# Layer 0: the second half's first norm moved to the start, the first half's output and cross attention moved beside the second half's attentions, the memories moved

## The chip, the core and the metric

The kernel runs on one core of a Trainium2 chip. Five engines work side by side and meet only through semaphores: PE (matmuls, with its weight loads PEld), DVE (vector work), ACT (activations), POOL (GpSimd) and SP, which here only issues DMAs. Each engine takes its instructions strictly in the order in which they stand in its queue. The metric is the device time of one execution in microseconds (us).

## What is computed

Two layers of a decoder for 1024 tokens of width 1024, all in fp32. What matters here is layer 0, cut to its main lines:

```python
x = x + mixers[0](rms_norm(x, mix_norm))                   # w_in, two attentions, w_out
x = x + memory_cross_attention(rms_norm(x, x_norm), rms_norm(mem, mem_norm), wq, wkv, wo)
x = x + swiglu(rms_norm(x, ffn_norm), wg, wu, wd)
...
z = h @ w_in                                               # even_mixer
qa, ka, va, cq, ckv, kr = jnp.split(z, EVEN_SPLITS, axis=-1)
oa, _ = banded_attention(rope(qa), rope(ka), va, SWA_WINDOW - 1, sink=sinks)
qb = (rms_norm(cq, q_norm) @ w_uq)                         # q_nope, q_rope (rope'd)
kvb = (rms_norm(ckv, kv_norm) @ w_ukv)                     # k_nope, vb
ob = causal_mla_attention(q_nope, q_rope, k_nope, k_rope, vb)
return jnp.concatenate([oa, ob], axis=-1) @ w_out
```

The cross attention has 4 heads over 256 memory tokens. Layer 1 has another attention and the same cross attention and SwiGLU.

## The kernel before

**Halves and streams.** The tokens are worked in two halves of 512 (A, `hf` 0, and B, `hf` 1). A causal attention of half B needs the keys and values of half A, so A can run ahead of B. All of the code is recorded as Python generators that yield how much PE work they have just recorded, in units of one 128x512 matmul. `weave(main, fill, ratio)` (line 341, `g_weave` line 293) takes turns: for each unit of `main` it lets `fill` record `ratio` units; a `Gap(n)` in `main` asks for at least n units of `fill` there (it stands for a latency that something must cover), and `Until(cond)` lets `fill` run until a mark is set. A scheduler then orders each engine's queue, starting from the order of recording. `scaled(g, f)` multiplies what a generator yields by f, and `DENSE` (0.05) marks parts that need next to no fill.

There are two streams with buffers of their own: S (`self.S`, names that begin with s) for the latency-bound work, with 5 of the 8 PSUM banks, and D (`self.D`, names with d) for dense projections, with 3 PSUM banks, 2 raw weight buffers and 3 pairs of weight slots `wh`/`wl`. Every product is made of three matmuls: operands are split into a high and a low part. For a weight block (128x1024) SP loads `wr`, ACT copies it to `wh` (line 212), POOL subtracts to get `wl` (line 181). For activations DVE does the subtraction (`lo`, line 181).

**Names.** `proj0_units(hf)` (line 991) is the projection of layer 0 for one half: `w_in`, the two latent norms (lines 1037 and 1052 are their two matmuls with ones), `w_ukv`, `w_uq`. `g_swa(hf)` (line 1210) is the sliding-window attention: scores line 1254, transposes 1278, values 1285 and 1286. `g_mla(hf)` (line 1309) with `g_heads` (line 822) is the latent attention of 8 heads: scores 749, softmax on DVE 758 to 767 and ACT 762, transposes 785, values 796 to 799. `g_rest(l, hf)` (line 881) is what follows: `w_out` (names `oh`, `ol`), a norm, the cross attention (`xq`, lines 942 to 968), `w_xo`, and the norm for the FFN. `g_accum` (line 645) adds each 128x512 product to x on DVE (line 660). `memory_units(l)` (line 564) makes keys and values of the memory for layer l (`mxn`, `mem`). `norm_b` (in `body`) is half B's first norm: load `xB`, squares on ACT, reciprocal root on DVE, `xn` on DVE (line 416), 32 transposes on PE (line 399). `g_ffn` (line 676) is the SwiGLU (`hfh`, `hfl`; DVE lines 687, 691, 181 and 660).

**Order of layer 0 before.** Two weaves.

1. `sparse`: `g_swa(0)`, `norm_b`, `g_mla(0)`, `g_rest(0, 0)`, all on S, with `dense` as fill on D: `proj0_units(0)` with the first two of the memory units of layer 0 inside it, the rest of these, then, after half B's norm, `proj0_units(1)` and the memory units of layer 1.
2. `first0`: `g_swa(1)`, `g_mla(1)`, `g_rest(0, 1)` on S, with half A's `g_ffn(0)` as fill on D at 1.6.

Layer 1 follows in two more weaves with the FFN of the other half as fill, and half B's last FFN runs alone.

Of the kernel before, what the change touches and what calls it, by code (L numbers as in the profile page):

```python
# [18 lines left out]
P = 128  # L19
# [24 lines left out]
R0, R1, R2, R3, R4 = 1.5, 1.6, 1.6, 2.3, 2.1  # L44
# [118 lines left out]
class Builder:  # L163
# [400 lines left out]
    def memory_units(self, l, s):  # L564
# [5 lines left out]
        def load():  # L570
            for b in range(2):
                xn.append(self.A4.tile([P, D], F32, tag="a4", name="mxn"))
                nc.sync.dma_start(xn[b], I["mem"][0, b * P:(b + 1) * P, :])
            return self.gain(f"l{l}_mem_norm")
# [14 lines left out]
        def norm(_):  # L589
# [3 lines left out]
            for b in range(2):  # L593
                yield from self.g_turn(s if l else self.S, xn[b], lambda k0: tuple(t[:, k0:k0 + 4, b * P:(b + 1) * P] for t in mv))
# [227 lines left out]
    def g_heads(self, s, m, hf, heads, bias, scale):  # L822
# [5 lines left out]
        def flush():  # L828
# [6 lines left out]
            if g % 2:  # L835
                self.att_out(m, ot, self.OTd[row0:row0 + 64, hf * 512:(hf + 1) * 512])
# [21 lines left out]
    def att_mem(self, hf, ext, rope, sets=None):  # L858
# [14 lines left out]
        if rope:  # L873
            m.qr = ring(2, 512) if hf else Ring([ext.tile([P, 512], F32R, name=f"qr{i}") for i in range(2)])
        m.ph = Ring([ext.tile([P, 512], F32R, name=f"ph{i}") for i in range(2)])
# [5 lines left out]
    def g_rest(self, l, hf, x, xsrc, out):  # L881

        nc, I, st, s = self.nc, self.I, self.st, self.S
        ts = slice(hf * 512, (hf + 1) * 512)
        if x is None:
            x = self.xtile("x")
            with self.hold(HOLD):
# [5 lines left out]
        def out_proj():  # L893
            with ExitStack() as es:
                o = self.pool(es, f"op{l}{hf}", 2)
                for c in range(4):
                    h = o.tile([P, 1024], F32R, tag="oh", name="oh")
                    lo = o.tile([P, 1024], F32R, tag="ol", name="ol")
                    with self.hold(HOLD):
                        self.split_in(s, h, lo, [(lambda raw: raw.rearrange("p (k t) -> p k t", t=512),  # L900
                                                  self.OTd[c * 256:(c + 1) * 256, ts].rearrange("(k p) t -> p k t", p=P))], "dve", nc.gpsimd)
# [3 lines left out]
        yield from self.scaled(out_proj(), DENSE)  # L905
# [4 lines left out]
        with ExitStack() as es:  # L910
# [9 lines left out]
            yield from self.scaled(self.units([q_unit(h) for h in range(4)]), DENSE)  # L920
# [51 lines left out]
            s.apart = True  # L972
# [9 lines left out]
            for c in range(2):  # L982
                yield from self.scaled(self.g_accum(s, [(q[:, 2 * c + j, 0], q[:, 2 * c + j, 1]) for j in range(2)],
                                                    I[f"l{l}_w_xo"], c * 256, x, after if c else None), DENSE)
# [6 lines left out]
    def proj0_units(self, hf, tab, s, given, mem=None):  # L991
# [190 lines left out]
        first = s if mem is None else self.S  # L1182
        qa = [(cols(pr * P), roped(self.to_queries(pr, hf), first if pr < 2 else s)) for pr in range(4)]
        if mem is None:
            yield cols(640), va
        yield cols(512), roped(self.to_keys(0, hf), first)
        if mem is not None:
            yield next(mem)
        yield from qa[0:2]
        if mem is not None:  # L1190
            yield next(mem)
# [12 lines left out]
        yield sq  # L1204
        yield q_nope(0)
# [562 lines left out]
```

## Time and profile before

| | us |
|---|---|
| median of 3 runs | 2974.36 (2972.03 to 2979.24) |
| the profiled execution, whole | 2978.69 |
| its span in the profile | 2976.7 |
| PE busy | 2819.6 (95%) |
| PEld, DVE, POOL, ACT busy | 2350.7, 1790.7, 1478.8, 1309.3 |
| granted PE clock, mean over the span | 0.973 |

The profile is one execution. "Busy" counts the time in which an engine has an instruction under way; matmuls overlap, so PE busy is not PE at its peak. The granted clock is 1.0 at 2.4 GHz and 0.5 at 1.2 GHz; a mean between says for what share of the stretch each was granted. A row of waits names the instruction that waited, and what came last of what it waited for.

### The profile page before, as it was taken

What the parts mean: (1) busy time and instruction counts of PE and PEld (TensorE: products, weight loads), DVE (VectorE), ACT (ScalarE), POOL (GpSimd) and SP (SyncE); (2) the same over time, 40 slices, a digit from 0 to 9 for tenths busy, and PEclk for the clock granted to TensorE, in tenths of its full rate; (3) what the DMA queues carried; (4) which work ended last, traced back from release to release, by engine and by line L of the source; (5) the groups of instructions that cost most, each with busy time, mean ns of one, the idle gap of its engine ahead of it and who ended that gap; (6) DMA issues with size and microseconds to landing.
All of it is one profiled execution on the core that took longest, in us unless ns stands there. A gap on an engine that the chain in (4) does not pass through costs nothing. (4 is left out here: it accounts for less than half of the span.)

```text
span 2976.7 us, 37929 instructions
## 1 busy us (share of the span) xinstructions
PE 2819.6 (95%) x13500; PEld 2350.7 (79%) x13500; DVE 1790.7 (60%) x3668; ACT 1309.3 (44%) x2539; POOL 1478.8 (50%) x1070
## 2 busy tenths in 40 slices
PE   6878998899999999999999999999999999999998
PEld 5666777787888887888888787877888878788887
DVE  5784766566765556346776646346888765652234
ACT  4654534454443343265544334356655533432222
POOL 3475544663444444554656344455665644444442
PEclk9987999999999999999999999999999999999999
DMA  5665644643434323464555333465555443333331
GB/s 168 179 209 175 210 140 133 165 142 106 143 122 132 122 86 123 136 203 152 160 151 174 106 107 107 141 199 169 170 157 148 154 144 111 92 121 99 92 100 63
DMA packets 385216, 417.61 MB, mean 140 GB/s; under 512 B 32964, under 2 KB 295364, under 8 KB 385028
## 3 DMA queue, kind: packets, MB, share of 16 engines
q1 hardware_dynamic: 333124, 245.67, 27.9%
q0 software_dynamic: 51904, 169.52, 17.3%
q8 instruction: 107, 1.75, 0.2%
q14 instruction: 81, 0.66, 0.1%
HBM read 347.09 MB, written 68.03 MB: 139 GB/s over the span
## 5 line engine op out<-in xcount | busy, mean ns | idle before, releaser
L181 POOL TENSOR_TENSOR wl<-wr,wh 128x1024 fp32r<-128x1024 f32 (+1 forms) x430 | 1039.6, 2425 | 913.6 <-ACT wh L212 864.1
L212 ACT ACTIVATE wh<-wr 128x1024 fp32r<-128x1024 f32 (+1 forms) x418 | 440.1, 1056 | 738.9 <-PE d L236 248.2
L236 PE MATMUL d<-hfh,wh 128*128 128x512 f32 x1408 | 559.1, 398 | 5.8 <-DVE x L660 5.8
L236 PE MATMUL d<-hfh,wl 128*128 128x512 f32 x1408 | 553.9, 394 | 0.0
L236 PE MATMUL d<-hfl,wh 128*128 128x512 f32 x1408 | 553.4, 393 | 0.0
L236 PE MATMUL d<-wh,a 128*128 128x512 f32 x1440 | 528.3, 398 | 10.4 <-DVE ra L360 3.0
L660 DVE TENSOR_TENSOR x<-d,x 128x512 f32<-128x512 f32 x344 | 234.3, 687 | 299.8 <-PE d L236 298.8
L236 PEld LDWEIGHTS d<-wh,a 128*128 128x128 f32 x1440 | 272.4, 190 | 69.4 <-issue 6.6
L236 PEld LDWEIGHTS d<-hfh,wh 128*128 128x128 f32 x1408 | 266.7, 189 | 55.2 <-issue 4.4
L236 PEld LDWEIGHTS d<-hfh,wl 128*128 128x128 f32 x1408 | 265.7, 189 | 53.0
L236 PEld LDWEIGHTS d<-hfl,wh 128*128 128x128 f32 x1408 | 266.5, 189 | 49.5
L236 PE MATMUL d<-wl,a 128*128 128x512 f32 x720 | 283.2, 395 | 0.0
L660 DVE TENSOR_TENSOR x<-s,x 128x512 f32<-128x512 f32 x192 | 130.6, 689 | 113.1 <-PE s L236 111.8
L181 DVE TENSOR_TENSOR a<-t,a 128x512 fp32r<-128x512 f32 x104 | 164.3, 1580 | 31.2 <-ACT a L693 28.4
L236 PEld LDWEIGHTS d<-wl,a 128*128 128x128 f32 x720 | 136.9, 190 | 24.3
L762 ACT ACTIVATE af<-af,nm 128x512 f32<-128x512 f32 (+3 forms) x160 | 94.1, 589 | 110.5 <-DVE nm L758 100.3
L181 DVE TENSOR_TENSOR pl<-s,ph 128x512 fp32r<-128x512 f32 (+1 forms) x158 | 97.7, 631 | 46.7 <-ACT ph L184 46.0
L184 ACT ACTIVATE ph<-s 128x512 fp32r<-128x512 f32 (+1 forms) x158 | 83.9, 551 | 83.7 <-PE s L785 80.1
L687 DVE SCALAR_TENSOR_TENSOR t<-t,d 128x512 f32<-128x512 f32 x88 | 60.2, 684 | 98.3 <-ACT t L686 97.8
L236 PE MATMUL s<-hmh,wl 128*128 128x512 f32 x256 | 100.7, 393 | 3.9 <-POOL wl L181 3.9
L399 PE MATMUL s<-ident,xn 128*128 128x128 f32 x384 | 62.8, 310 | 41.9 <-DVE xn L416 39.1
L236 PE MATMUL s<-hml,wh 128*128 128x512 f32 x256 | 100.3, 392 | 0.0
(360 smaller groups left out, 5690.3 us busy)
## 6 DMA issues: line engine op xcount, KB each, us to landing
wr<-in_l_w_gate SPq DMA_DIRECT2D x88, 512.0 KB
wr<-in_l_w_up SPq DMA_DIRECT2D x88, 512.0 KB
wr<-in_l_w_down SPq DMA_DIRECT2D x88, 512.0 KB
wr<-in_l_w_qkv SPq DMA_DIRECT2D x48, 512.0 KB
wr<-in_l_w_out SPq DMA_DIRECT2D x32, 512.0 KB
tab<-qd POOLq DMA_DIRECT2D x32, 512.0 KB, 5.6
ar<-qd POOLq DMA_DIRECT2D x24, 512.0 KB, 7.4
wr<-in_l_w_in SPq DMA_DIRECT2D x22, 512.0 KB
```

What stands on the lines that cost most here:

```text
L181: e.tensor_sub(out, x, h.bitcast(F32))
L184: self.nc.scalar.activation(h, ps, AF.Copy)
L212: self.nc.scalar.activation(h, raw, AF.Copy)
L236: self.nc.tensor.matmul(ps, a, b, start=(3 * i + j == 0), stop=(3 * i + j == n - 1))
L399: self.nc.tensor.transpose(v[:, k, :], xn[:, (k0 + k) * P:(k0 + k + 1) * P], self.ident)
L660: self.nc.vector.tensor_add(xs, ps, xs)
L687: nc.vector.scalar_tensor_tensor(t, t, 1.0, pg, op0=ALU.add, op1=ALU.mult)
L762: nc.scalar.activation(p[:, c:c + n], p[:, c:c + n], AF.Exp, bias=nm, scale=-1.0, accum_out=l[:, i:i + 1])
```

## The change

Layer 0 is cut into its two weaves at another place. What was said of layer 1 and of the last FFN is unchanged.

- `norm_b` is recorded at the very start, beside the first units of `proj0_units(0)`, with `Gap(6)` ahead of it and gaps of 12 between its blocks (8 before).
- The memory units of layer 0 leave `proj0_units(0)`. Their load and norm come four units before the end of `proj0_units(1)`, their products behind it. Those of layer 1 head the fill of the second weave. Both use D alone, and two tiles of the pool `xn` for the memory.
- `g_rest(0, 0)` leaves the main stream of the first weave. It runs as fill on D in the second weave, behind layer 1's memory units and ahead of half A's FFN, beside `g_swa(1)` and `g_mla(1)`; on D its dense parts count in full (`dense` 1.0) and it holds no DMA back (`held` None).
- The ratios: 2.0 (was 1.5) for `g_swa(0)`, 2.8 (was 1.6) for `g_mla(0)`, 2.1 (was 1.6) for the second weave. `g_rest(0, 1)` waits by `Until` for half A's to be recorded.
- `g_mla` starts once the first 4 heads' queries are marked and waits for the second mark before head 4; `q_rope` comes ahead of `q_nope`. The first loads of `g_swa(1)` are issued ahead of the last values of `g_mla(0)` (`ahead`). The attention's output tensor is split into one per half. Weight slots of S, free in these stretches, hold queries, keys' rope part, bias and the split probabilities of the attentions; the names `ph`, `pl`, `qr` become `pp`, `wh`, `wl` there.

```diff
-R0, R1, R2, R3, R4 = 1.5, 1.6, 1.6, 2.3, 2.1
+R0, R1, R2, R3, R4 = 2.0, 2.8, 2.1, 2.3, 2.1
...
-    def g_heads(self, s, m, hf, heads, bias, scale):
+    def g_heads(self, s, m, hf, heads, bias, scale, need={}, last=None):
...
+                    if i + 1 in need:
+                        yield need[i + 1]
                     nxt = heads[i + 1][0]()
+        if last:
+            last()
         yield Gap(12)
...
-    def g_rest(self, l, hf, x, xsrc, out):
-
-        nc, I, st, s = self.nc, self.I, self.st, self.S
+    def g_rest(self, l, hf, x, xsrc, out, s=None):
+
+
+        nc, I, st = self.nc, self.I, self.st
+        held = HOLD if s is None else None
+        dense = DENSE if s is None else 1.0
+        s = s or self.S
...
         def norm_b():
-            gB = self.gain("l0_mix_norm")
-            h, dst = self.new_acts("hB")
+            yield Gap(6)
             xB = self.xtile("xB")
             for tb in range(4):
                 nc.sync.dma_start(xB[tb], x_in[512 + tb * P:512 + (tb + 1) * P, :])
-            yield from self.g_norm_T(S_, xB, gB, dst, 20, 8)
+            h, dst = self.new_acts("hB")
+            yield from self.g_norm_T(S_, xB, g, dst, 20, 12)
             hB.append(h)
...
         def dense():
-            m0 = self.memory_units(0, D_)
-            yield from self.proj0_units(0, tab, D_, [hA], m0)
-            yield from m0
+            yield from self.proj0_units(0, tab, D_, [hA])
             tabB = self.big("tabB", F32)
             tabs(tabB, 1)
             yield (lambda: None), wait
-            m1 = self.memory_units(1, D_)
-            yield from self.proj0_units(1, tabB, D_, hB)
-            yield from m1
-
-        def sparse(nxt):
+            m0 = self.memory_units(0, D_)
+            us = list(self.proj0_units(1, tabB, D_, hB))
+            yield from us[:-4]
+            yield next(m0)
+            yield from us[-4:]
+            yield from m0
+
+        def sparse():
+            yield from norm_b()
             yield Until(lambda: ("swa", 0, 0) in self.done)
             yield from self.scaled(self.g_swa(0), R0)
-            yield from norm_b()
-            yield Until(lambda: ("mla", 0) in self.done)
-            yield from self.scaled(self.g_mla(0), R1)
-            yield from self.scaled(self.g_rest(0, 0, None, x_in, nxt), R1)
+            yield Until(lambda: ("mla", 0, 0) in self.done)
+
+            def ahead():
+                g = self.g_swa(1)
+                swa.extend([next(g), g])
+
+            yield from self.scaled(self.g_mla(0, ahead), R1)
+
+        swa = []
+        self.weave(sparse(), self.units(dense()), 1.0)
...
+        def rest_and_ffn():
+            x = self.xtile("x")
+            for tb in range(4):
+                nc.gpsimd.dma_start(x[tb], x_in[tb * P:(tb + 1) * P, :])
+            yield from self.units(self.memory_units(1, D_))
+            yield from self.g_rest(0, 0, x, None, fA, D_)
+            self.done.add(("rest", 0))
+            yield from self.g_ffn(0, *fA, D_)
+
+        def second(nxt):
+            yield swa[0]
+            yield from swa[1]
+            yield from self.g_mla(1)
+            yield Until(lambda: ("rest", 0) in self.done)
+            yield from self.g_rest(0, 1, None, x_in, nxt)
```

**SP's queue in the first 60 us**, with half B's load (`xB`), the tables' store and load (`tabs`, `tab`) and the memory (`mxn`). Before:

```order
L452 DMA tabc<-in_positions 128x1x128
L210 DMA wr<-in_l_w_in 128x8x128 x2
L347 DMA g<-in_l_mem_norm 128x1024
L573 DMA mxn<-in_mem 128x1024 x2
L210 DMA wr<-in_l_w_in 128x8x128
L487 DMA tabs<-tabc 4x32x256 x2
L489 DMA tabs<-tabc 8x16x128 x2
L494 DMA tab<-tabs 128x1x512 x4
```

After, from the same row of the positions on:

```order
L452 DMA tabc<-in_positions 128x1x128
L210 DMA wr<-in_l_w_in 128x8x128 x3
L487 DMA tabs<-tabc 4x32x256 x2
L489 DMA tabs<-tabc 8x16x128 x2
L494 DMA tab<-tabs 128x1x512
L210 DMA wr<-in_l_w_in 128x8x128
L494 DMA tab<-tabs 128x1x512 x3
L1682 DMA xB<-in_x 128x1024 x4
```

The memory's two loads have left this place, and half B's four stand there, behind the tables' loads instead of ahead of them.

**PE's queue where D turns to half B** (`hB` half B's activations, `mem` the memory's products, `ar` and `qr` operands of the attentions, `pp` probabilities). Before, it is inside `g_mla(0)`:

```order
L785 MATMUL s<-ident,af 128x128 x2
L628 MATMUL d<-wl,mem 128x512
L628 MATMUL d<-wh,mem 128x512 x2
L628 MATMUL d<-wl,mem 128x512
L628 MATMUL d<-wh,mem 128x512
L628 MATMUL d<-wl,mem 128x512
L628 MATMUL d<-wh,mem 128x512 x2
L628 MATMUL d<-wl,mem 128x512
L628 MATMUL d<-wh,mem 128x512
L236 MATMUL d<-hBh,wh 128x512
L236 MATMUL d<-hBl,wh 128x512
L796 MATMUL s<-ph_1728,ar 128x256
```

After, it is inside `g_swa(0)`:

```order
L236 MATMUL d<-a_1411,wh 128x512 x2
L236 MATMUL d<-a_1411,wl 128x512
L1306 MATMUL s<-pp_674,kv_680 128x512
L1307 MATMUL s<-pp_676,kv_680 128x512
L1306 MATMUL s<-pp_675,kv_680 128x512
L1299 MATMUL s<-ident,af 128x128 x4
L1307 MATMUL s<-pp_677,kv_680 128x512
L1299 MATMUL s<-ident,af 128x128 x4
L236 MATMUL d<-hBh,wh 128x512
L236 MATMUL d<-hBl,wh 128x512
L236 MATMUL d<-hBh,wl 128x512
```

The memory's products no longer stand between the two halves, and half B's projection begins before the latent attention of half A does.

**DVE's queue inside `g_mla(1)`** (`af` the probabilities, `x<-d,x` the addition of a product of D to x, `t` and `a` the FFN's). Before, with the FFN as fill:

```order
L767 TENSOR_SCALAR af<-af,rl 128x768
L660 TENSOR_TENSOR x<-d,x 128x512
L181 TENSOR_TENSOR pl_5653<-s,ph_5651 128x512
L181 TENSOR_TENSOR pl_5654<-s,ph_5652 128x384
L758 ISA af,nm<-s,bias 128x512
L758 ISA nm 128x1
L660 TENSOR_TENSOR x<-d,x 128x512
L687 SCALAR_TENSOR_TENSOR t_6915<-t_6915,d 128x512
L758 ISA af,nm<-s,bias,nm 128x384
L758 ISA nm 128x1
L764 TENSOR_TENSOR l<-l 128x1
L766 RECIPROCAL rl<-l 128x1
```

After, with `w_out` of half A as fill:

```order
L767 TENSOR_SCALAR af<-af,rl 128x896
L660 TENSOR_TENSOR x<-d,x 128x512
L181 TENSOR_TENSOR ol<-wr,oh 128x1024
L660 TENSOR_TENSOR x<-d,x 128x512
L758 ISA af,nm<-s,wl,nm 128x512
L758 ISA nm 128x1
L819 TENSOR_TENSOR af<-s,af 64x512
L660 TENSOR_TENSOR x<-d,x 128x512
L764 TENSOR_TENSOR l<-l 128x1
L766 RECIPROCAL rl<-l 128x1
L660 TENSOR_TENSOR x<-d,x 128x512
L767 TENSOR_SCALAR af<-af,rl 128x1024
```

Between two blocks of the softmax there now stand two or three additions to x, each for 6 matmuls of `w_out`, where one stood with the FFN's own steps.

## Rows read from the trace of the kernel before

**Rows 1.** The page's parts 1 and 2: busy time by engine, and the span in 40 slices of 74.4 us (PE busy in tenths of a slice; PEclk is the granted clock in tenths).

```profile
PE 2819.6 (95%) x13500; PEld 2350.7 (79%) x13500; DVE 1790.7 (60%) x3668; ACT 1309.3 (44%) x2539; POOL 1478.8 (50%) x1070
...
PE   6878998899999999999999999999999999999998
...
PEclk9987999999999999999999999999999999999999
```

**Rows 2.** Busy time by stretch: us from A to B, its length, then busy us (and instructions) of PE, PEld, DVE, ACT and POOL, the granted clock, DMA share and GB/s. Start; rest of the first weave; the two attentions of half B beside the FFN; the rest of the second weave.

```profile
0.00:94.00 94.00, 67.77 (x320) 58.44 (x320) 59.05 (x123) 42.69 (x72) 33.50 (x30) 0.93 0.62 177
94.00:577.00 483.00, 411.18 (x1934) 333.91 (x1933) 320.32 (x690) 234.01 (x482) 261.26 (x241) 0.90 0.56 171
577.00:925.00 348.00, 339.22 (x1766) 287.43 (x1765) 225.01 (x493) 166.97 (x359) 163.96 (x131) 0.98 0.43 132
925.00:1203.00 278.00, 272.39 (x1273) 224.83 (x1272) 164.52 (x297) 105.28 (x180) 125.43 (x61) 0.99 0.37 115
```

**Rows 3.** PE's timeline, start and duration: the first full matmul of half A's projection, then the first and the last of 57 in a row that wait for nothing.

```profile
39.14 0.45 PE L236 MATMUL s<-hAh,wh 128*128 128x512 f32 x1
...
42.65 0.39 PE L236 MATMUL s<-hAh,wh 128*128 128x512 f32 x1
...
55.34 0.39 PE L236 MATMUL s<-hAh,wl 128*128 128x512 f32 x1
```

**Rows 4.** Who PE waited for from 0 to 575 us: total us, times, longest.

```profile
PE s L399 <- DVE xn L416: 27.5, 10, 9.0
PE d L1052 <- DVE t L1046: 11.8, 4, 4.6
PE s L796 <- ACT ph L184: 9.1, 6, 4.1
PE s L399 <- DVE mxn L586: 8.9, 2, 7.6
PE s L968 <- DVE wl L181: 7.6, 2, 4.8
```

**Rows 5.** Busy time by stretch, columns as in rows 2: around half B's norm and the start of `g_mla(0)`, cross attention of half A, its last norm.

```profile
180.00:213.00 33.00, 24.52 (x155) 21.68 (x154) 26.91 (x31) 15.43 (x26) 26.17 (x29) 0.91 0.70 209
213.00:270.00 57.00, 41.80 (x159) 32.61 (x159) 30.29 (x80) 20.36 (x50) 31.12 (x45) 0.68 0.71 208
...
460.00:510.00 50.00, 38.91 (x191) 31.78 (x190) 36.83 (x48) 23.02 (x57) 23.31 (x17) 0.90 0.47 153
...
556.00:577.00 21.00, 12.65 (x59) 10.16 (x58) 15.84 (x30) 6.10 (x10) 12.35 (x14) 0.76 0.81 200
```

**Rows 6.** Groups of instructions on DVE and PE from 577 to 925 us: line, operation, tile, shapes, count, then busy us and mean ns, and idle time before them. The attention's largest, the FFN's four, and the FFN's five matmul groups.

```profile
L181 DVE TENSOR_TENSOR pl<-s,ph 128x512 fp32r<-128x512 f32 (+1 forms) x72 | 46.5, 656 | 19.5 <-ACT ph L184 19.0
L660 DVE TENSOR_TENSOR x<-d,x 128x512 f32<-128x512 f32 x51 | 34.9, 688 | 20.0 <-PE d L236 19.8
...
L181 DVE TENSOR_TENSOR a<-t,a 128x512 fp32r<-128x512 f32 x14 | 22.1, 1576 | 9.8 <-ACT a L693 9.7
...
L1256 DVE CUSTOM_DVE_ANT_0 s<-s,af,nsink 128x256 f32<-128x256 f32 x32 | 15.1, 489 | 7.1 <-PE s L1254 4.5 <-ACT af L1259 2.5
...
L687 DVE SCALAR_TENSOR_TENSOR t<-t,d 128x512 f32<-128x512 f32 x15 | 10.3, 684 | 17.6 <-ACT t L686 17.5
...
L691 DVE SCALAR_TENSOR_TENSOR t<-t,d 128x512 f32<-128x512 f32 x14 | 9.6, 683 | 2.4 <-PE d L236 2.4
...
L236 PE MATMUL d<-hfl,wh 128*128 128x512 f32 x228 | 90.8, 398 | 0.0
L236 PE MATMUL d<-hfh,wh 128*128 128x512 f32 x225 | 90.7, 403 | 4.0 <-DVE x L660 4.0
L236 PE MATMUL d<-hfh,wl 128*128 128x512 f32 x227 | 90.5, 400 | 0.0
L236 PE MATMUL d<-wh,a 128*128 128x512 f32 x204 | 79.3, 405 | 0.0
L236 PE MATMUL d<-wl,a 128*128 128x512 f32 x102 | 40.9, 401 | 0.0
```

**Rows 7.** Groups on DVE from 350 to 575 us: the largest of `g_rest(0, 0)`.

```profile
L660 DVE TENSOR_TENSOR x<-s,x 128x512 f32<-128x512 f32 x48 | 32.7, 689 | 25.8 <-PE s L236 25.3 <-DMA wr<-OTd 0.2
L416 DVE SCALAR_TENSOR_TENSOR xn<-x,rr,g 128x1024 f32<-128x1024 f32 x8 | 11.3, 1413 | 0.0
...
L181 DVE TENSOR_TENSOR ol<-wr,oh 128x1024 fp32r<-128x1024 f32 x4 | 7.8, 1955 | 9.1 <-ACT oh L212 9.1
...
L942 DVE TENSOR_REDUCE nm<-s 128x2 f32<-128x512 f32 x8 | 5.4, 679 | 6.1 <-PE s L236 6.1
...
L181 DVE TENSOR_TENSOR hfl<-s,hfh 128x512 fp32r<-128x512 f32 x8 | 5.3, 682 | 0.9 <-ACT hfh L184 0.9
```

**Rows 8.** Busy time by stretch, columns as in rows 2: where DVE was busiest for 200 us (layer 1's attention of half B) and for 50 us (behind it), and half A's two attentions in layer 0.

```profile
2110.00:2310.00 200.00, 194.55 (x1043) 168.96 (x1042) 166.92 (x420) 115.53 (x301) 121.61 (x112) 0.99 0.53 160
...
2580.00:2630.00 50.00, 45.97 (x211) 37.90 (x210) 47.51 (x127) 20.70 (x40) 19.03 (x8) 0.97 0.43 131
...
94.00:345.00 251.00, 205.87 (x977) 166.44 (x976) 169.41 (x401) 137.04 (x304) 145.92 (x156) 0.88 0.62 192
```

**Rows 9.** The timeline at the start, start and duration: SP's issue of the tables' loads, and DVE's first instruction that needs the second table.

```profile
50.41 3.26 SPq L494 DMA_DIRECT2D tab<-tabs  x4
...
61.93 0.69 DVE L507 TENSOR_TENSOR t<-s,tab 128x512 f32<-128x512 f32 x1 [5.54 <-DMA tab<-tabs]
```

**Rows 10.** Groups on POOL from 690 to 920 us, inside `g_mla(1)`.

```profile
L181 POOL TENSOR_TENSOR wl<-wr,wh 128x1024 fp32r<-128x1024 f32 x28 | 68.6, 2455 | 93.1 <-ACT wh L212 93.0
```

More of the change, by code (lines that the diff above doesn't have):

```diff
@@ L593, in norm @@
             for b in range(2):
-                yield from self.g_turn(s if l else self.S, xn[b], lambda k0: tuple(t[:, k0:k0 + 4, b * P:(b + 1) * P] for t in mv))
+                yield from self.g_turn(s, xn[b], lambda k0: tuple(t[:, k0:k0 + 4, b * P:(b + 1) * P] for t in mv))
         w = I[f"l{l}_w_xkv"]
@@ L918, in q_unit @@
                 return lambda: self.wcols(s, I[f"l{l}_w_xq"], h * P), f
-            yield from self.scaled(self.units([q_unit(h) for h in range(4)]), DENSE)
+            yield from self.scaled(self.units([q_unit(h) for h in range(4)]), dense)
             kv = self.big("mkv")
@@ L983, in g_rest @@
                 yield from self.scaled(self.g_accum(s, [(q[:, 2 * c + j, 0], q[:, 2 * c + j, 1]) for j in range(2)],
-                                                    I[f"l{l}_w_xo"], c * 256, x, after if c else None), DENSE)
+                                                    I[f"l{l}_w_xo"], c * 256, x, after if c else None), dense)
         g = self.gain(f"l{l}_ffn_norm")
@@ L1215, in g_swa @@
         with ExitStack() as es:
-            ext = self.pool(es, f"sw{hf}", 1)
-            r = Carve([self.big("ar") for _ in range(1 + hf)])
             c = Carve([self.big("af", F32)])
-            q = Ring([r.take(2048).rearrange("p (h t) -> p h t", h=4) for _ in range(2)])
+            if hf:
+                r = Carve([self.big("ar") for _ in range(2)])
+                q = Ring([r.take(2048).rearrange("p (h t) -> p h t", h=4) for _ in range(2)])
+                (h, l) = s.slot()
+                pp = [x[:, i:i + 512] for x in (h, l) for i in (0, 512)]
+            else:
+                ext = self.pool(es, f"sw{hf}", 1)
+                q = Ring([[x.rearrange("p (h t) -> p h t", h=2) for x in s.slot()] for _ in range(2)])
+                pp = [ext.tile([P, 512], F32R, name=f"pp{i}") for i in range(4)]
             pr = Ring([c.take(1024).rearrange("p (h k) -> p h k", k=256) for _ in range(2)])
@@ L1331, in head @@
                 return f
-            yield from self.g_heads(s, m, hf, [(head(hd), 512 + 64 * hd) for hd in range(8)], m.bias, SC96)
+            yield from self.g_heads(s, m, hf, [(head(hd), 512 + 64 * hd) for hd in range(8)], m.bias, SC96,
+                                    {4: Until(lambda: ("mla", hf, 1) in self.done)}, last)
     def sets1(self, tab, hf):
@@ L1600, in build @@
         self.ident = const.tile([P, P], F32, name="ident")
-        self.OTd = dram.tile([D, S], F32, name="OTd")
+        self.OTd = [dram.tile([D, 512], F32, name=f"OTd{hf}") for hf in range(2)]
         xd = dram.tile([S, D], F32, name="xd")
```

73 lines of the change are left out of this document (38 added, 35 removed).

## The prediction

> **What bounds the kernel now.** I read the page first: PE is busy 95% of the span, and its row of slices shows where it is not. From slice 17 on there are only 8s and 9s; the 6s, 7s and the low clocks stand in the first eight slices [rows 1], which is the first weave of layer 0. The stretches put numbers to it [rows 2]. From 0 to 577 us PE was busy 67.77 + 411.18 = 479 us, so 98 us were idle. The granted clock was 0.93 and 0.90; at the 1.2 GHz level matmuls take twice as long, so a mean clock c costs (1 - c) of the time PE works: 0.07 x 67.8 + 0.10 x 411 = 46 us. Together 144 us lost, and 433 us of work at full clock. From 577 to 1203 us, beside the FFN, idle is 8.8 + 5.6 us and the clock costs 0.02 x 348 + 0.01 x 278 = 9.8 us: 24 us lost, 602 us of work. So the first weave holds what layer 0 can give, and the change neither adds nor removes a matmul: 433 + 602 = 1035 us of work must be done before layer 1 starts, at 1203 us now.
>
> What the idle time waits for is short chains [rows 4]: transposes for normed activations (27.5 us for `xn`, 8.9 for `mxn`), the latent norms (11.8), split probabilities (9.1), cross attention (7.6). At half B's norm and behind it D has nothing but the memory's products, so that PE was busy 24.5 of 33 and 41.8 of 57 us and the clock was 0.68; in half A's cross attention it was busy 38.9 of 50, in its last norm 12.7 of 21 [rows 5]. These are places where one latency-bound chain runs with too little beside it.
>
> DVE is the other number to watch. Up to 577 us it was busy 59.05 + 320.32 = 379 us, no less a share (66%) than in the FFN's stretch (225.01 of 348, 65%) [rows 2].
>
> **The change, part by part.**
>
> *Norm of half B at the start.* It removes the waits of `xn` in the stretch from 180 us and lets half B's projection follow half A's at once. It adds at the start 4 loads, 4 squares, a reciprocal root, 4 `xn` and 32 transposes, and takes out the memory's 2 loads, 4 half squares, 2 `mxn` and 16 transposes. Its loads stand on SP behind the tables' loads, which were issued from 50.4 to 53.7 us and of which the second was in at 61.9 us [rows 9]. So `xn` is ready between some 66 us (the loads overlap the tables') and 77 us (they come after: 2.1 MB at the 177 GB/s of [rows 2] are 12 us, then a root and 1.4 us for `xn` [rows 7]), while PE gets there at about 66 us (120 full matmuls stand ahead, from 39.1 us on, [rows 3]): its wait lies between 0 and 11 us. There is such a wait now, 7.6 us for `mxn` [rows 4]. I take it as equal, net 0 (from -8 to +3). Behind the waiting transposes on PE stand the second query projection and the first scores.
>
> *The memories and the ratios* move work that is dense on D. They cost nothing of their own on PE; their DVE work (8 to 9 us each) is in the counts below.
>
> *`g_rest(0, 0)` beside half B's attentions.* This is the main gain, and it moves a limit. The idle of 11 + 8 us in its cross attention and last norm [rows 5] gets `g_mla(1)` or half B's `w_out` as cover. But `g_mla(1)`, which had the FFN beside it, gets work that is as rich in DVE as itself.
>
> *What must be done until `g_mla(1)` ends.* In the changed order that is the first weave less half A's last norm, and half B's two attentions, without a matmul of the FFN.
> - PE: the FFN's 986 matmuls from 577 to 925 us [rows 6] at (55.34 - 42.65) / 56 = 0.2266 us [rows 3] are 223 us. The attentions are the rest, 348 - 8.8 idle - 7.0 clock - 223 = 109 us. With 433 and less 3.5 for 32 transposes: 538 us of PE work.
> - DVE: 379 us, and of the 225 in half B's stretch all but the FFN's 34.9 + 22.1 + 10.3 + 9.6 = 77 us [rows 6], so 148; less 11 for half A's last norm (half of `xn`, 11.3 / 2, and 5.3 for `hfl`) [rows 7]. That is 516 us of DVE work.
>
> So DVE, not PE, has nearly as much to do as the stretch can last. The first 94 us are much as before (59 us of DVE). The other 457 us of DVE run at some rate u, and PE then has 1035 - 538 = 497 us left, beside half B's `g_rest` and the FFN, where it lost 8.4 of 278 us [rows 2]: 497 x 1.03 = 512 us. Layer 1 starts at 94 + 457 / u + 512, against 1203 now. No gain is left at u = 0.766.
>
> *Which u.* Below is 0.66, DVE's mean from 94 to 577 us [rows 2], where one latency-bound chain ran at a time. Above is 0.95, reached for 50 us. Between lies 0.835, over 200 us, with PE busy 97% beside it [rows 8]: the only long stretch in which a softmax on DVE and dense work kept both busy. I take that row, since the stretch to come is long and mixed like it. 457 / 0.835 = 548; 94 + 548 + 512 = 1154, a gain of 49 us.
>
> Against this stands a rule on the port that DVE and POOL share. The additions that read PSUM took 688 ns, while `a<-t,a`, with both inputs in SBUF, took 1576 ns for the same shape [rows 6], and `ol` 1955 ns [rows 7]; POOL's splits took 2455 ns each [rows 10]. The Trainium skill (SBUF — State Buffer, section "Who interferes with whom") says that a DVE instruction with two SBUF inputs contends with a GpSimd instruction that reads SBUF, and that the loser is blocked for the whole instruction; the rows agree. Taken at its worst, the 4 `ol` and 4 `xn` of half A would each wait for one more split, 8 x 2.455 = 20 us, and the sum would be a gain of 49 - 20 / 0.835 = 25 us. I leave that out of the sum: POOL has 16 splits beside this part of half A, fewer than the 28 it had in 230 us of the FFN.
>
> **The sum.** The profiled execution took 2978.7 us (span 2976.7). 2978.7 - 49 = 2929.7. It lies 4.3 us above the median of the runs, 2974.4, so I predict 2925 us for a median.
>
> **The rivals.**
>
> *DVE does not bind; PE is as full as beside the FFN.* Then PE loses 8.8 + 7.0 of 348 us, 4.5%, over the whole stretch: 63 us of its work are done at 94 us, the other 475 take 475 / 0.955 = 497 us, and layer 1 starts at 94 + 497 + 512 = 1103: a gain of 100, 2874 us. DVE would have to run at 457 / 497 = 0.92 for 500 us. For it: most of DVE's idle time in [rows 6] is waiting for PE and ACT, which a second chain fills. Against it: above 0.9 DVE was seen for no more than 50 us [rows 8].
>
> *Slower: two softmax chains get in each other's way in `g_mla(1)` beside `g_rest(0, 0)`.* This stage has about 200 us of DVE work: 148 less some 36 for `g_swa(1)` (15.1 for its masked minimum, 16 of 72 `pl`, small ones) [rows 6], and about 89 of `g_rest(0, 0)` (57 in [rows 7], with `hxl` as `hfl`, and about 32 of splits and roots). At 0.835 that is 240 us. PE's queue is one: a head of cross attention that waits for DVE (waits of up to 4.8 us, [rows 4]) now holds up the scores of `g_mla(1)` behind it, and D has 3 PSUM banks where S had 5. If DVE gets 0.66 there, as in [rows 2] from 94 us, the stage takes 303 us, and 63 us more than the gain of 49 makes 14 us slower, 2988 us. It decides below 200 / (240 + 49) = 0.69.
>
> *Nothing comes of it.* If DVE's rate over the whole stretch is between 0.755 and 0.775, the time is within 9 us of now. The rate of half A's two attentions, 169.41 / 251 = 0.675 [rows 8], is below that, so a small rise alone brings nothing: the waits at PE's chains would have turned into waits for DVE.
>
> **How the numbers follow.** A measurement of this kernel can tell about 0.3%, 9 us, from no change. The forecast (a gain of 9 to 75 us, u from 0.775 to 0.87) has 0.58; the first rival (more than 75) 0.16; no change 0.10; slower 0.16, for the second rival and for a start that waits the full 11 us and a DVE near the lower bound. Faster is 0.58 + 0.16 = 0.74, same 0.10, slower 0.16. The range leaves out a tenth at either side: from a gain of 90 (u near 0.91) to a loss of 10 (u near 0.75), 2884 to 2984 us.
>
> **What would show it.** In the changed profile layer 1's first projection should start near 1154 us on the span, where it stood near 1203. The stretch from 94 us to the last value matmul of `g_mla(1)`, near 640 us, should show DVE at 0.83 and PE at some 0.87 with a clock above 0.95, and no stretch of 50 us with a clock below 0.8 behind the start. The waits of PE for `xn` should fall from 27.5 us to below 20, since half A's last norm has half B's `w_out` beside it; the wait at the first transposes of half B at about 66 us stays. I am wrong if DVE is busy less than 0.77 there, if PE waits for something else than DVE in `g_mla(1)` (weights, or a POOL queue that waits), or if time is lost behind 1203 us, where I take nothing to change.

## The result, and the profile after

The changed kernel took 2994.23 us, median of 4 runs (2988.35 to 2998.07), the one before 2975.98 (4 runs): a ratio of 1.0055, 95% interval 1.0043 to 1.0067. It is slower by 16 us, where 2925 was forecast. The profiled run took 2998.07 us; its span, its busy times and slices:

```profile
span 2996.3 us, 37866 instructions
PE 2811.4 (94%) x13500; PEld 2340.8 (78%) x13500; DVE 1793.1 (60%) x3668; ACT 1306.8 (44%) x2539; POOL 1478.6 (49%) x1074
PE   6888779989999999999999999999999999999998
DVE  5778757887354534346776636346888756652234
PEclk9899889999999999999999999999999999999999
```

The 7 of [rows 1] has moved, not gone: the third slice is an 8 now, but the fifth and sixth (300 to 450 us), which were 9s before, are 7s. Busy time, granted clock, DMA share and GB/s by stage, against [rows 2, 5]:

```profile
0.00:94.00 94.00, 62.19 (x305) 53.43 (x306) 52.12 (x97) 39.73 (x64) 32.10 (x28) 0.93 0.62 172
94.00:213.00 119.00, 98.82 (x445) 78.11 (x446) 95.27 (x208) 71.27 (x161) 69.03 (x65) 0.91 0.60 174
213.00:360.00 147.00, 124.13 (x609) 101.42 (x607) 107.98 (x261) 83.47 (x176) 75.55 (x94) 0.93 0.59 176
360.00:475.00 115.00, 84.04 (x483) 71.44 (x484) 66.44 (x158) 54.14 (x131) 84.54 (x86) 0.88 0.79 237
475.00:700.00 225.00, 203.05 (x1130) 171.15 (x1128) 187.83 (x451) 130.35 (x305) 90.00 (x85) 0.98 0.41 132
94.00:700.00 606.00, 510.04 (x2663) 422.12 (x2663) 457.52 (x1074) 339.23 (x771) 319.13 (x330) 0.94 0.56 171
```

The columns are PE, PEld, DVE, ACT and POOL busy. From 475 to 700 us `g_mla(1)` runs beside `g_rest(0, 0)`, and DVE is busy 187.83 / 225 = 0.835, the very rate of [rows 8]. The hole is ahead of it: from 360 to 475 us, where half B's projection is done and `g_swa(1)` has only the products of the two memories beside it, PE is idle for 31 us and the clock costs 0.12 x 84 = 10 more. DVE is busy 0.58 there. PE's waits at the start (from 0 to 105 us), then in that stretch, then DVE's longest in it:

```profile
PE s L399 <- DVE xn L416: 14.0, 3, 9.0
PE d L236 <- ACT wh L212: 11.3, 1, 11.3
PE d L1049 <- DVE t L1041: 7.0, 1, 7.0
...
PE d L399 <- DVE mxn L586: 11.4, 1, 11.4
PE d L236 <- DVE a L181: 8.7, 1, 8.7
...
DVE mxn L586 <- DMA mxn<-in_mem: 12.9, 1, 12.9
```

The first is nearly all half A's own norm and stood there before (13.6 us). The second is order on ACT's queue: the copy of D's next weights (L212) stands behind the square of half B's x (L372), whose load stands behind the tables' on SP.

```profile
66.44 0.63 ACT L527 ACTIVATE a<-t 128x512 fp32r<-128x512 f32 x1 [12.65 <-issue]
70.23 1.06 ACT L372 ACTIVATE xn<-xB 128x1024 f32<-128x1024 f32 x1 [3.15 <-DMA xB<-in_x]
71.19 0.18 ACT L372 ACTIVATION_READ_ACCUMULATOR xn<-xB 128x1 f32 x1
71.28 1.04 ACT L212 ACTIVATE wh<-wr 128x1024 fp32r<-128x1024 f32 x1
```

Layer 1's first projection starts at 1221.4 us, and before at 1206.4 (the prediction took 1203). The row of the changed kernel, then of the one before:

```profile
L1409 PE MATMUL s<-wh,hmh x64: 389/389/390, 1221.4 to 1279.7; 128*128 128x512 f32 x64
L1387 PE MATMUL s<-wh,hmh x64: 389/389/389, 1206.4 to 1264.6; 128*128 128x512 f32 x64
```

From there to the end it is 1775 and 1770 us: 15 of the 20 us by which the two profiled spans differ were lost in layer 0, the other 5 behind it, for a reason that was not looked for.

### The profile page after: what moved, and what is told of

Read it like the earlier page. It is cut to its first block, busy times and chain, and to the rows that moved or that the text cites. A ratio compares the mean times of both kernels' runs of the same rounds, so it can differ in the third digit from the quotient of the medians.

```text
span 2996.3 us, 37866 instructions
## 1 busy us (share of the span) xinstructions
PE 2811.4 (94%) x13500; PEld 2340.8 (78%) x13500; DVE 1793.1 (60%) x3668; ACT 1306.8 (44%) x2539; POOL 1478.6 (49%) x1074
## 5 line engine op out<-in xcount | busy, mean ns | idle before, releaser
L181 POOL TENSOR_TENSOR wl<-wr,wh 128x1024 fp32r<-128x1024 f32 (+2 forms) x430 | 1038.5, 2423 | 933.6 <-ACT wh L212 884.4
L212 ACT ACTIVATE wh<-wr 128x1024 fp32r<-128x1024 f32 x418 | 440.1, 1056 | 850.0 <-PE d L236 356.6
L660 DVE TENSOR_TENSOR x<-d,x 128x512 f32<-128x512 f32 x392 | 266.6, 686 | 388.4 <-PE d L236 387.1
L181 DVE TENSOR_TENSOR a<-t,a 128x512 fp32r<-128x512 f32 x104 | 151.4, 1456 | 33.8 <-ACT a L693 27.6
L660 DVE TENSOR_TENSOR x<-s,x 128x512 f32<-128x512 f32 x144 | 97.4, 687 | 84.2 <-PE s L236 82.8
L687 DVE SCALAR_TENSOR_TENSOR t<-t,d 128x512 f32<-128x512 f32 x88 | 60.2, 685 | 108.9 <-ACT t L686 108.5
L236 PE MATMUL s<-hmh,wh 128*128 128x512 f32 x256 | 99.9, 390 | 0.2 <-ACT wh L212 0.2
L767 DVE TENSOR_SCALAR af<-af,rl 128x384 f32<-128x384 f32 (+7 forms) x128 | 94.3, 748 | 1.8
L691 DVE SCALAR_TENSOR_TENSOR t<-t,d 128x512 f32<-128x512 f32 x88 | 60.0, 682 | 58.9 <-PE d L236 58.6
```

The costliest lines, as they stand in the source:

```text
L181: e.tensor_sub(out, x, h.bitcast(F32))
L212: self.nc.scalar.activation(h, raw, AF.Copy)
L236: self.nc.tensor.matmul(ps, a, b, start=(3 * i + j == 0), stop=(3 * i + j == n - 1))
L660: self.nc.vector.tensor_add(xs, ps, xs)
L687: nc.vector.scalar_tensor_tensor(t, t, 1.0, pg, op0=ALU.add, op1=ALU.mult)
L691: nc.vector.scalar_tensor_tensor(t, t, 0.5, pu, op0=ALU.mult, op1=ALU.mult)
```

## Experiments

Each time is a median, with its ratio to the kernel before (95% interval) from runs on one chip. "By the ratios" means the difference of two such ratios times 2976 us. Kernels e9 to e11 multiply the last block of `g_swa(1)`'s first key group by the second group's values; the work is the same.

**The waits one by one.** e1 moves four loads, e2 one load to another queue:

```diff
+            yield from self.units(self.memory_units(1, D_))
             for tb in range(4):
                 nc.gpsimd.dma_start(x[tb], x_in[tb * P:(tb + 1) * P, :])
-            yield from self.units(self.memory_units(1, D_))
```

> The changed kernel, with the four loads of half A's x (2 MB, on POOL's queue at the head of the second weave) issued behind layer 1's memory units instead of ahead of them. Nothing else is moved by hand. Theory 1 (crowded transfers between the weaves: from 360 to 405 us the DMA engines are busy 93 to 103%, and loads that land in 4 to 7 us elsewhere take 17): the memory's load for layer 1 lands near 380 instead of 388 us, PE's wait of 8.7 us at 392 falls below 3, half B's first scores come some 8 us before 394.7, and the time falls by 6 to 10 us, to about 2986. Theory 2 (the chain of the memory's norms through DVE, with nothing else recorded for PE there): the 11.4 us at 370 stay in any case, the 8.7 us too, and the time stays within 3 us of 2994.

3001.79, 1.0082 (1.0066 to 1.0097): neither. The wait of 8.7 us fell to 6.1, no more: the DMA engines are as full without these 2 MB (share 1.02 and 1.03 from 370 to 390 us). What it lost, behind 475 us, was not followed further.

```diff
-            nc.sync.dma_start(m.bias, I["c_mla"][:, S - W:])
+            (nc.sync if hf else nc.gpsimd).dma_start(m.bias, ...)
```

> The changed kernel, with the load of the mask of g_mla(0) issued from POOL's queue instead of SP's. Theory (queue order: the mask's buffer is free only when g_swa(0) has read its last probabilities at 217.3 us, and D's next two weight loads stand behind it on SP): the weights come some 8 us earlier, PE's wait of 8.9 us at 230 falls below 4, and the time falls by 4 to 9 us, to about 2988. Rival (the scores of g_mla(0) wait for their own operands, which need the same buffers): D's work is done earlier and PE then waits just as long for the same scores; total idle from 205 to 360 us and the time stay within 3 us.

2993.76, 1.0058 (1.0043 to 1.0072): the rival. D's work came earlier and PE waited for the same scores.

e3 takes the four loads of `xB` out of `norm_b` and puts them ahead of `self.tables()`:

> The changed kernel, with half B's x loaded ahead of the tables on SP's queue. Theory (order on ACT's queue: the copy of D's next weights stands behind the square of half B's x, which is in only at 70.2 us): PE's wait of 11.3 us at 72.4 goes, the stretch from 0 to 105 us loses some 34 us instead of 45, and the time falls by 7 to 11 us, to about 2985. Rival (the start is bound by one chain after the other, so the next one takes over: the first scores wait for queries that need the tables, the latent norm for DVE): the wait comes back within 105 us, and the time falls by less than 4 us.

2981.56, 1.0020 (1.0010 to 1.0031): 10 us by the ratios, as the theory said.

e4 puts `m0` back: `proj0_units(0, tab, D_, [hA], m0)`, then `yield from m0`.

> The changed kernel, with layer 0's memory units back in half A's projection and behind it, as before the change; layer 1's stay at the head of the second weave. Theory (what was lost between the weaves, some 48 us from 360 to 475, is the memory's norms and products with too little beside them): the loss between the end of half B's projection and the first scores of g_mla(1) falls to some 25 us, the first weave gets 22 us of work longer but loses no more, and the time falls by 15 to 20 us, to about 2977. Rival (the memory's products wait for their weights, 2.4 us of POOL for 2.8 us of PE each, wherever they stand): the loss moves with them into the first weave, and the time stays within 5 us of 2994.

3016.68, 1.0134 (1.0114 to 1.0155): both wrong; 22 us slower. The memory inside half A's projection is worse than between the weaves.

**The stretch between the weaves, on top of e3.** e5 takes the memory's load and norm earlier (`us[:-7]`, `us[-7:-4]`, `us[-4:]` with `next(m0)` between); e6 adds `yield Gap(40)` ahead of the first head of `g_mla(0)`; e7 swaps `memory_units(1)` and `g_rest(0, 0)`; e8 leaves the second norm out (`if l == 0: yield load, prep; yield ..., norm`).

> The kernel of e3, with the load of layer 0's memory seven units before the end of half B's projection (it was four) and its transposes four units before the end (they stood behind the last). Theory (between the weaves PE has nothing to do but the memory's transposes, which wait for their norm; 11.1 us at 358 and, behind them, 6.1 us at 377 for a split that stands on DVE behind the norm of layer 1's memory): with the transposes ahead of the last projections the first wait goes and the second shrinks, and the time falls by 8 to 15 us from the 2981.6 of e3, to about 2970, below the kernel before. Rival (half B's first scores set the time: they wait for their operands till about 382, whatever PE does meanwhile): the waits move to the products' end, the first scores still come near 382 us, and the time falls by less than 4 us.

> The kernel of e3, with a gap of 40 units of fill ahead of the first scores of g_mla(0) (9 us of half B's projection recorded there). Theory (PE waits 7.6 us at 217 for these scores' operands, which are loaded only when g_swa(0) has freed their buffers): the wait falls below 2 us, and the time falls by 4 to 8 us from 2981.6, to about 2976. Rival (the latent attention's own chain sets the end of the first weave, and what fills one wait is missing in a later one): the wait goes, idle time comes up behind it by as much, and the time stays within 3 us.

> The kernel of e3, with layer 1's memory units behind g_rest(0, 0) instead of ahead of it, so that half A's w_out is what stands beside the end of the first weave and g_swa(1). Theory (the memory's norm and its products, with two loads, 8 weight blocks and 10 stores of little PE work each, are a poor cover for g_swa(1); from 360 to 475 us POOL was busy 84 of 115): PE's loss there falls from some 45 to some 25 us, and the time falls by 10 to 20 us, to about 2967. Rival (g_swa(1) with its two short chains, masked minimum on DVE and a product on POOL, is the slow part, whatever D does): the stretch loses as much with w_out beside it, and the time stays within 5 us of 2981.6.

> The kernel of e3 without the second norm of the memory: layer 1's memory units take layer 0's normed memory (its loads, products on DVE, 16 transposes and 8 splits are left out, so layer 1's gain is missing from the output). PE's own work falls by 1.6 us. Theory (the norm's chain load, DVE, transposes, splits holds up the products of both memories: DVE waits 12.9 us for its load, with layer 0's splits behind that): the wait of 6.1 us at 377 goes and the time falls by 6 to 12 us, to about 2973. Rival (the products' weights and POOL set the pace of the memories): the time falls by 1 to 4 us only.

e5 2981.04, 1.0009 (0.9999 to 1.0018): the rival's time, but not its course. The wait at 358 us went, and the scores of `g_swa(1)` ran from 355 to 427 us where they ran from 381 to 442 in e3; PE then waited 11.2 us for weights, and nothing was gained. So an early `g_swa(1)` alone does not shorten the stage. e6 2975.41, 0.9992 (0.9983 to 1.0000): theory, 8 us by the ratios. e7 2971.80, 0.9982 (0.9973 to 0.9991): a gain, at the theory's lower end. e8 2978.83, 1.0010 (1.0001 to 1.0019): the rival, 3 us of which 1.6 are the work left out. No single wait is the whole cause: most of what these four take away at one place is waited for at the next.

**`g_swa(1)`'s operands early (e9), with memory 1 late (e10), with e5 and e6 as well (e11).**

```diff
-                r = Carve([self.big("ar") for _ in range(2)])
-                q = Ring([r.take(2048).rearrange(...) for _ in range(2)])
+                r = Carve([self.big("ar")])
+            q = Ring([[...] for x in s.slot()] for _ in range(2)])
...
+                    if last and i + 1 == 5:
+                        last()
```

> The kernel of e3, with the operands of g_swa(1) in buffers that are free earlier (queries in S's weight slots, the rest in one buffer instead of two, one value buffer instead of two), so that they are loaded behind the operands of head 5 of g_mla(0) instead of behind the last head's. Theory (between the weaves 10 MB of loads keep the DMA engines full from some 350 to 395 us, and g_swa(1), the memory and D's weights all wait for them): with 2.6 MB of it moved ahead the stretch is at 1.0 for a shorter time, the first scores of g_swa(1) come right behind g_mla(0), near 355 instead of 382 us, and the time falls by 10 to 20 us from 2981.6, to about 2967. Rival (g_swa(1) is slow by its own chain through DVE, ACT and POOL): its first scores come earlier, its last no more than 5 us earlier, and the time falls by less than 5 us.

> e9 with layer 1's memory units behind g_rest(0, 0), as in e7. Theory (two separate loads on the same stretch, transfers and the memory's products): the gains add up, 10 us of e7 and what e9 gives: about 2957. Rival (either one takes the stretch to the pace of g_swa(1)'s chain, where nothing more is to be had): no faster than the better of e7 and e9 by more than 3 us.

> e10 with the gap of e6 ahead of g_mla(0) and the memory's earlier norm of e5. Theory (each of these waits is a place of its own): another 4 to 8 us from the gap, about 2951. Rival (the first weave ends when the latent attention's chain ends): within 3 us of e10.

e9 2968.30, 0.9967 (0.9954 to 0.9979): the theory's time, but by the trace the rival's course: the first scores came at 324 us, the last at 446.0 (442.1 in e3). e10 2953.82, 0.9917 (0.9904 to 0.9931): the gains add up, as the theory said, and the last scores come at 421. The scores of `g_swa(1)` in e3, e5, e9 (two rows) and e10 (its last row):

```profile
L1275 PE MATMUL s<-ar x64: 277/283/562, 381.0 to 442.1; 128*128 128x256 f32 x64
L1275 PE MATMUL s<-ar x64: 278/283/389, 355.2 to 427.2; 128*128 128x256 f32 x64
L1274 PE MATMUL s<-ar,wh x32: 279/283/580, 324.0 to 445.5; 128*128 128x256 f32 x32
L1274 PE MATMUL s<-ar,wl x32: 278/283/385, 341.4 to 446.0; 128*128 128x256 f32 x32
L1274 PE MATMUL s<-ar,wl x32: 278/283/385, 340.0 to 421.4; 128*128 128x256 f32 x32
```

With the memory out of the way the early operands count. e11 2968.02, 0.9962 (0.9949 to 0.9976), is slower than e10 by 14 us, against theory and rival; its last scores came earlier still, at 412 us. Which of its two additions costs was not separated.

**One part at a time.** e12 undoes the move of `g_rest(0, 0)` on e3. With it go the new places of the memories (layer 0's stand behind half A's projection, neither inside it as before nor at the end of half B's; layer 1's behind half B's projection) and all three ratios:

```diff
-            yield from self.scaled(self.g_mla(0, ahead), R1)
+            yield from self.scaled(self.g_mla(0), R1)
+            yield from self.scaled(self.g_rest(0, 0, None, x_in, fA), R1)
...
-            yield Until(lambda: ("rest", 0) in self.done)
+R0, R1, R2, R3, R4 = 1.5, 1.6, 1.6, 2.3, 2.1
```

> One part of the change alone: half B's norm at the start (its x loaded early, as in e3), but g_rest(0, 0) back in the main stream of the first weave, g_swa(1) and g_mla(1) beside half A's FFN, the memories behind their halves' projections, and the ratios of before. Theory A (moving g_rest(0, 0) took the FFN away from g_swa(1) and gave it the memories: the move lost more than it gained): faster than e3, about 2965, since the stretch of half B's norm (45 us lost of 90 before) is gone and the rest is as before. Theory B (the move of g_rest(0, 0) gains what the forecast said, 27 us lost in its cross attention and norm, and the stretch between the weaves is an accident of its own): slower than e3 by 10 to 20 us, about 2995, since cross attention has only the memory beside it.

2941.21, 0.9870 (0.9856 to 0.9883): theory A, and 24 us beyond it; layer 1 starts at 1164.6. Of the next four, e13 and e14 change the first two ratios of e3 and e12, e15 and e16 one place in e12.

> The kernel of e3 (g_rest(0, 0) beside half B's attentions) with 1.5 and 1.6 for g_swa(0) and g_mla(0), as before the change, instead of 2.0 and 2.8. Theory A (the move itself costs: what is left to stand beside half B's attentions is too little, and what is left for later is too much): the time stays within 10 us of 2981.6. Theory C (the ratios cost: they use up half B's projection beside g_mla(0)): the time falls by 20 us or more, to below 2962.

> The kernel of e12 (g_rest(0, 0) in the main stream of the first weave) with 2.0 and 2.8 for g_swa(0) and g_mla(0), as after the change, instead of 1.5 and 1.6; 1.6 stays for the second weave. Theory A (the move itself): within 10 us of 2941. Theory C (the ratios): slower by 20 us or more, above 2961, since half B's projection is used up ahead of g_rest(0, 0).

> The kernel of e12 with half B's x loaded where the change loads it, behind the tables. Theory (the wait of 11.3 us at 72 us is a separate price, as in e3, where its removal gave 12 us): 8 to 13 us slower than e12, about 2951, still 20 us or more faster than the kernel before. Rival (where the first weave has enough to do the wait is hidden): within 4 us of 2941.

> The kernel of e12 with the first two of layer 0's memory units inside half A's projection, as before the change, instead of behind it. Theory (the memories' places are worth little where half A's norm, w_out and the FFN stand where they stood): within 6 us of 2941. Rival (the memory behind the projection is what made e12 fast): slower by 15 us or more.

e13 2985.57, 1.0031 (1.0020 to 1.0043): theory A. e14 2974.78, 0.9992 (0.9983 to 1.0000): theory C. Both hold, each on its own kernel: the two ratios cost 34 us (36 by the ratios to before) where `g_rest(0, 0)` stands in the first weave and nothing where it was moved. What theory A calls the move is more than `g_rest(0, 0)`: e13 differs from e12 also in the memories' places and in the third ratio. e15 2948.85, 0.9908 (0.9892 to 0.9923): theory, 8 us of it (11 by the ratios). e16 2963.79, 0.9954 (0.9939 to 0.9969): the rival, 23 us. Stretches of e12, then e13, then e14:

```profile
205.00:360.00 155.00, 136.68 (x694) 115.11 (x695) 98.31 (x231) 82.84 (x165) 95.76 (x108) 0.92 0.65 203
360.00:580.00 220.00, 205.80 (x1016) 172.22 (x1015) 142.14 (x318) 103.50 (x211) 115.98 (x85) 0.96 0.54 159
580.00:700.00 120.00, 120.00 (x617) 101.26 (x616) 80.58 (x181) 59.29 (x134) 64.84 (x55) 1.00 0.45 140
700.00:925.00 225.00, 223.15 (x1158) 189.40 (x1157) 148.91 (x287) 101.42 (x193) 95.36 (x74) 0.99 0.41 129
```

```profile
205.00:360.00 155.00, 126.20 (x626) 102.67 (x624) 117.37 (x289) 89.43 (x196) 85.91 (x107) 0.93 0.69 201
360.00:580.00 220.00, 188.64 (x1071) 160.29 (x1071) 159.54 (x408) 119.99 (x273) 125.55 (x129) 0.94 0.57 186
580.00:700.00 120.00, 107.66 (x595) 90.37 (x595) 86.58 (x210) 65.10 (x151) 44.68 (x37) 0.99 0.38 126
700.00:925.00 225.00, 220.04 (x977) 182.21 (x978) 103.50 (x171) 65.24 (x98) 92.01 (x43) 0.98 0.33 103
```

```profile
205.00:360.00 155.00, 127.62 (x649) 109.27 (x650) 91.77 (x222) 79.80 (x162) 85.70 (x95) 0.88 0.58 179
360.00:580.00 220.00, 190.90 (x889) 154.81 (x889) 122.67 (x273) 89.97 (x167) 107.26 (x84) 0.93 0.52 158
```

Idle time plus (1 - clock) x busy, as in the prediction: e12 loses 29 + 22 + 0 + 4 us, e13 38 + 43 + 13 + 9. The 48 us more stand for the 44 between the two (the clocks are means to 0.01). e14 loses 43 + 42 in the first two, 34 more than e12: the 34 between them. For the memory's place, e16 and then e12:

```profile
94.00:194.00 100.00, 75.65 (x342) 59.45 (x341) 72.05 (x170) 51.02 (x127) 46.99 (x45) 0.85 0.44 120
194.00:294.00 100.00, 70.86 (x365) 60.35 (x364) 50.05 (x114) 39.38 (x81) 62.26 (x76) 0.81 0.71 209
```

```profile
94.00:194.00 100.00, 78.67 (x358) 61.34 (x356) 85.28 (x194) 59.21 (x144) 59.21 (x55) 0.91 0.58 166
194.00:294.00 100.00, 82.93 (x468) 72.11 (x468) 57.97 (x158) 49.10 (x109) 63.43 (x84) 0.91 0.73 213
```

78 us lost against 53: 25 more, which are the 23 measured, beside `g_swa(0)` and the first heads of `g_mla(0)`. Which of e16's waits there (11.2 us for its softmax, 10.9 for weights, 8.9 for queries) begins it was not settled.

> The kernel of e12 with 2.0 for g_swa(0) instead of 1.5; 1.6 stays for g_mla(0) and g_rest(0, 0). Theory (the second ratio, which uses half B's projection up beside g_mla(0), makes the 34 us of e14): within 8 us of 2941. Rival (the first ratio: with 2.0 half A's projection and the memory are used up ahead of g_mla(0)): slower by 15 us or more.

> The kernel of e12 with 1.2 for g_mla(0) and g_rest(0, 0) instead of 1.6. Theory (what is left of half B's projection behind g_mla(0) is the best cover that g_rest(0, 0) can have; from 2.8 to 1.6 it gave 34 us): the stretch from 360 to 580 us, which lost 27 us in e12, loses less than 20, and the time stays the same or falls by up to 10 us, as far as g_mla(0) itself does not lose what is gained. Rival (1.6 is already past the point from which g_mla(0) lacks cover): slower by 8 us or more, lost between 205 and 360 us.

e17 2938.17, 0.9865 (0.9850 to 0.9880): the theory; it is the second ratio. This median is the lowest of all, but 3 us below e12 is less than these runs can tell. e18 2955.08, 0.9921 (0.9907 to 0.9934): slower as the rival said, but not where it said:

```profile
360.00:460.00 100.00, 96.61 (x451) 79.12 (x451) 69.68 (x145) 43.88 (x79) 49.38 (x35) 1.00 0.51 149
460.00:580.00 120.00, 91.77 (x444) 75.48 (x443) 59.05 (x138) 47.98 (x104) 55.73 (x45) 0.87 0.46 139
```

`g_rest(0, 0)` now ends first, and layer 1's memory units run behind it with nothing beside them (from 525 us, until the FFN begins at 557). By this run the two streams of this weave should end together.

## Why the prediction was wrong

**The counts held, the rate did not.** The sum was 94 + 457 / u + 512. DVE's work from 94 to 700 us is 457.52 us, as worked out. The last value matmul of `g_mla(1)` starts 7.5 us later, and 512 more make 1219.5; it was 1221.4.

```profile
707.52 0.33 PE L799 MATMUL s<-wl,ar 128*128 128x256 f32 x1
```

The step that failed is "Which u": the forecast took 0.835 for the whole of it, "since the stretch to come is long and mixed like it". Only its last 225 us were. The rates by stage are 95.27 / 119 = 0.80, 107.98 / 147 = 0.73, 66.44 / 115 = 0.58 and 0.835; over 606 us 0.755, below the break-even of 0.766 that the prediction named. DVE was not full in the first three. From 94 to 213 us PE waited longest for a step of a latent norm (7.0 us), from 213 to 360 us for the operands of the first scores of `g_mla(0)` (8.9), from 360 us for the norm of layer 0's memory (11.4), then for a split (8.7) that stood on DVE behind the norm of layer 1's, which waited 12.9 us for its load. Taking one engine's rate from a place where it binds, for stages where single chains and loads do, was the error. At 0.835 the 606 us would have been 548; of the 58 us the stretch from 360 us is 115 - 66.44 / 0.835 = 35, the one ahead of it 18, the first 5.

**Memories and ratios "cost nothing of their own on PE".** They were put at nothing, and each is of the size of the whole loss: layer 0's memory inside half A's projection instead of behind it costs 23 us (e16), and in the changed kernel taking it out of there gained 22 (e4); layer 1's memory as the cover of `g_swa(1)` costs 10 (e7); the second ratio costs 37 where `g_rest(0, 0)` was not moved (e14 against e17), and both new ratios together nothing where it was (e13 against e3). A product of the memory is little work for its weights; what was costed was PE's work, which is the same everywhere, and not what it leaves uncovered.

**Norm of half B at the start.** Its wait was put between 0 and 11 us, as a wait of the transposes for `xn`. It was 11.3 us, as a wait of the projection for its weights behind ACT's square; loading x first gives back 10 to 11 by the ratios (e3, e15). Together with the new place of layer 0's memory, and the other small edits, e12 is 39 us faster than the kernel before; with that memory back inside half A's projection 14 are left (e16), for the norm, its early loads and the small edits together.

**`g_rest(0, 0)` beside the attentions: "the main gain".** Moved together with the memories it costs 44 us with the old ratios (e13 against e12) and 8 with the new (e3 against e14). That is not the price of `g_rest(0, 0)` alone: with layer 1's memory behind it instead of ahead of it the moved kernel (e7) took 3 us less than e14. With the old ratios no run parts `g_rest(0, 0)` from the memories. What its cross attention and norm lose is 26 us before [rows 5], and still 22 in e12 over a longer stretch; that is all there was to win. Half B's attentions, which lost 16 us beside the FFN [rows 2], got in its place work that waits as they do.

**The rivals.** The slower one came true in its sign and not in its mechanism: in `g_mla(1)` DVE had 0.835, not 0.66. The rule of the Trainium skill that the prediction left out of its sum (SBUF — State Buffer, section "Who interferes with whom") would have made `ol` and `xn` longer. By the trace that price, 20 us at its worst, did not come: `ol` took 1436 ns where it took 1955 in [rows 7] (three took 1.2 us and one 2.1), `xn` 1698 where it took 1413, so that four of each come to 1 us less.

```profile
L181 DVE TENSOR_TENSOR ol<-wr,oh 128x1024 fp32r<-128x1024 f32 x4 | 5.7, 1436 | 0.0
L416 DVE SCALAR_TENSOR_TENSOR xn<-x,rr,g 128x1024 f32<-128x1024 f32 x5 | 8.5, 1698 | 0.0
```

**The tests named.** From 94 to 640 us DVE was busy 403.20 / 546 = 0.74, PE 0.83, with a clock of 0.93: each below what was named, and DVE below the 0.77 given as the mark of being wrong. PE's waits for `xn` on S fell from 27.5 to 14.0 us, as said, with 1.8 on D, where half A's last norm now stands. That time would be lost behind layer 1's start was named as a mark too, and 5 us were.

**In the place of the theory** stands cover: dense matmuls that wait for nothing new (a projection's tail, the FFN) fill the attentions' waits, and there is a fixed amount. That this is the cause is a reading of the stretches of e12, e13, e14 and e18; what the runs themselves show is what each place costs. Over e12 the move with the memories costs 44 us, the two ratios 34, both together 40 (e3): by this reading each takes the dense work from a latency-bound stage that needs it, and it can be taken only once. That the crowded loads between the weaves (below) are the reason for the stretch at 360 us is shown only in part: early operands gain 13 to 18 us by the medians, and do so fully only with the memory out of the way (e10).

## What to carry to other kernels

Before moving a latency-bound stage, list the dense work that covers each such stage now and after; a stage that gains cover takes it from another. A rate read at one place holds for another only if the same engine binds there, so ask stage by stage which wait ends last. Work that "costs nothing" on the busiest engine still has a place, and where it stands can be worth more than the change.

## What was not expected of the hardware

Between the weaves the DMA engines were full by their busy share while they moved a fifth to a quarter less than when they were as full 30 us later. After, in stretches of 10 us (DMA share and GB/s are the last two columns):

```profile
370.00:380.00 10.00, 9.28 (x60) 8.64 (x61) 4.48 (x6) 3.04 (x5) 5.13 (x9) 0.77 1.04 273
380.00:390.00 10.00, 3.58 (x30) 3.38 (x29) 1.53 (x1) 2.39 (x5) 3.40 (x4) 0.92 1.02 293
390.00:400.00 10.00, 7.11 (x34) 6.50 (x35) 7.69 (x21) 3.32 (x15) 6.85 (x8) 0.57 1.04 271
400.00:410.00 10.00, 8.54 (x59) 7.47 (x58) 6.63 (x18) 5.79 (x17) 6.72 (x6) 1.00 0.97 366
```

Full meant 273 GB/s in one stretch and 366 in another. Among what was under way from 365 to 400 us are `g_swa(1)`'s queries (64 partitions, rows of 2 KB), which landed 16.9 us after their issue, and half A's x on the same queue (128 partitions, rows of 4 KB), which took as long:

```profile
ar<-qd POOLq DMA_DIRECT2D x4, 512.0 KB, 16.9
x<-in_x POOLq DMA_DIRECT2D x4, 512.0 KB, 17.9
```

So the landing times do not single out the short rows; that they are the reason was not tried by itself. In e1, which loads x later, the engines were as full from 370 to 390 us at 269 and 240 GB/s, so x is not needed for it.
